# Value products of two successive attention steps issued in the same scheduler step

## The chip, the cores and the metric

The kernel runs on one core of one Trainium2 chip, in one launch. The metric is the device time of a run in microseconds (us); the lower the better. The engines are named as in the profile: PE is TensorE's matmul, PEld its weight load, DVE is VectorE, ACT is ScalarE, POOL is GpSimd, SP is SyncE.

## The reference, cut to what matters

Two encoder layers of width 1024 over 1024 positions. Layer 0 mixes by two groups of 8 heads of 64 value columns, latent attention (MLA) and stick-breaking attention; layer 1 mixes by 16 heads of chunked band attention. A SwiGLU block follows each mixer. Everything is float32. The change touches the three attentions alone:

```python
# MLA: block-causal softmax attention
p_a = softmax(where(chunk_ok, s_a, -inf));  out_a = p_a @ v_a

# stick-breaking: no softmax, a reverse running sum over the keys
log_keep = where(before, log_sigmoid(-z), 0)
log_between = cumsum(log_keep, reverse=True) - log_keep
w_b = where(before, exp(log_sigmoid(z) + log_between), 0);  out_b = w_b @ v_b

# band: own 64-wide chunk and the 8 chunks before it, with a learned bias
p = softmax(where(valid, scores + bias, -inf));  o = p @ v
```

## The kernel before, in words

Each attention handles two heads at once (index `e`) and half the positions at once (`hf`, 512 queries as the columns of a matmul). Along the keys it goes in steps of 128 (`j`): `sb_step`, `mla_attend` and `band_attend` each make one step per block of keys. On or near the diagonal a step covers 384, 256 or 128 of the 512 columns, and stick-breaking goes through the blocks from the last to the first.

A step has stages. Its first stage multiplies keys with queries (scores, in a two-bank PSUM tile `z`) and leaves exponentials in an SBUF tile `a`. Its last stage is the **value product**, `weighted` (L815 to L819): one matmul per head with the tile `a` as the moving operand and 64 value columns as the weights, so that the two heads write the two halves of the 128 partitions of one PSUM bank `o`, which collects all steps of a head pair and half. Stick-breaking has a middle stage, `weights()`: L904, L907 and L909 form the running sum on PE, DVE L915 subtracts it, ACT L916 takes the exponential. The softmax attentions add their exponentials into a tile `b` (L1060: POOL, for the last pairs DVE), and `soft_finish` ends a head pair and half: a matmul with ones for the denominators (L1076), ACT L1078 and L1079, DVE L1080, L1081 and L1082.

`step` holds a list of pending stages. Each call first issues the next stage of every earlier step, oldest first, then the first stage of its own. How many empty stages stand before the last one sets its **lag**: with `LAG` = 2 the weights of a stick-breaking step are issued two calls after its scores and its outputs two calls after that; a band value product is issued two calls after its scores, an MLA one four (`soft_step(2 * LAG, ...)`). Between calls `weave` issues a quota of **fill**: dense three-part matmuls of the next projections or of the output projection (L274, L275, L276), with their weight splits (`rest`, L242). `with_max` puts the row maxima of the next head pair between the steps (MLA: PE L1037, DVE L1039; band: PE L1163, DVE L1166; both end in `neg_max_rows`, L1018 and L1021).

The order in which the calls issue instructions is what the tile scheduler is given; the scheduler then sets the order on each engine, within the dependences and the buffers. Each engine runs its own order strictly from front to back. PSUM has two banks `mm` for fill, two pairs `z`, two banks `o`. The tile `a` has four buffers in layer 0 and three in the band.

In the trace stick-breaking lies between about 86 and 420 us, MLA between 430 and 650, the band between 1422 and 1896. The SwiGLU blocks and the projections around them make up the rest.

Of the kernel before, what the change touches and what calls it, by code (L numbers as in the profile page):

```python
# [30 lines left out]
LAG = 2  # L31
# [119 lines left out]
class Trunk:  # L151
# [711 lines left out]
    def sb_step(self, p, hf, j, proj, vt, st, o_d):  # L863
# [8 lines left out]
        cs = slice(c0, HALF)  # L872
# [55 lines left out]
                nc.sync.dma_start(o_d[hf][4 + p], ot)  # L928

        idle = [lambda: None] * (LAG - 1)  # L930
        self.step(scores, *idle, weights, *idle, outputs)

# [106 lines left out]
        self.neg_max_rows(m2, hf + 1, [qs[e][hf][0][96:100, :] for e in range(2)])  # L1041
        yield

    def soft_step(self, lag, scores, cs, st, vt, j, first, last, dest):
        x = {}

        def front():
            ex = x["ex"] = self.tmp("a")
            scores(ex)
            if first:  # L1050
                st["ex"] = ex
            else:
                old = st["ex"]
                if "esum" not in st:
                    st["esum"] = self.tmp("b")
                    if cs.start:
                        self.nc.scalar.copy(st["esum"][:, :, 0:cs.start], old[:, :, 0:cs.start])
                else:
                    old = st["esum"]
                self.eng("dve" if dest[2] else "pool").tensor_tensor(st["esum"][:, :, cs], old[:, :, cs], ex[:, :, cs],  # L1060
                                                                     ALU.add)

        def back():
            if first:
                st["o"] = self.out_bank()
            self.weighted(st["o"], vt, j, x["ex"], cs, first, last)
            if last:
                self.soft_finish(st["o"], st["esum"], *dest)

        self.step(front, *[lambda: None] * (lag - 1), back)  # L1070

    def soft_finish(self, o, esum, row, k, keep):
        nc = self.nc
# [16 lines left out]
    def mla_attend(self, p, hf, proj, vt, o_d):  # L1090
        nc = self.nc
        mm = nc.tensor.matmul
        qs, ks = proj
        st = {}
        nj = 4 * hf + 4
        for j in range(nj):
            kh, r = divmod(j, 4)
            bs = slice(r * P, (r + 1) * P)
            diag = kh == hf
            cs = slice(r * P if diag else 0, HALF)  # L1100
            kr = 104 if diag else 100

            def scores(ex, kh=kh, bs=bs, cs=cs, kr=kr):
                z = self.banks()
                for e in range(2):
                    qh, ql = qs[e][hf]
                    kth, ktl = ks[e][kh]
                    mm(z[:, e, cs], kth[0:kr, bs], qh[0:kr, cs], start=True, stop=False)  # L1108
                    mm(z[:, e, cs], kth[0:96, bs], ql[0:96, cs], start=False, stop=False)
                    mm(z[:, e, cs], ktl[0:96, bs], qh[0:96, cs], start=False, stop=True)  # L1110
                nc.scalar.activation(ex[:, :, cs], z[:, :, cs], AF.Exp, scale=96 ** -0.5)

            self.soft_step(2 * LAG, scores, cs, st, vt, j, j == 0, j == nj - 1, (o_d[hf], p, p == 3))
            yield 1.0 if not diag else 1.0 - 0.25 * r


# [56 lines left out]
    def band_attend(self, p, hf, proj, tk, vt, o_d):  # L1173
        nc = self.nc
        mm = nc.tensor.matmul
        qs, ks = proj
        st = {}
        order = [0, 1, 2, 3] if hf == 0 else [3, 4, 5, 6, 7, 2, 1, 0]
        for n, j in enumerate(order):
            kh, r = divmod(j, 4)  # L1180
            bs = slice(r * P, (r + 1) * P)
            i0, i1 = max(j, 4 * hf), min(j + 4, 4 * hf + 3)
            cs = slice((i0 - 4 * hf) * P, (i1 - 4 * hf + 1) * P)
            xs = slice((i0 - j) * P, (i1 - j + 1) * P)

            def scores(ex, kh=kh, bs=bs, cs=cs, xs=xs):
                z = self.banks()
                for e in range(2):
                    mm(z[:, e, cs], ks[e][kh][0][:, bs], qs[e][hf][0][:, cs], start=True, stop=False)  # L1189
                    mm(z[:, e, cs], ks[e][kh][1][0:68, bs], qs[e][hf][1][0:68, cs], start=False, stop=True)  # L1190
                nc.vector.tensor_tensor(ex[:, :, cs], z[:, :, cs], tk[:, :, xs], ALU.add)  # L1191
                nc.scalar.activation(ex[:, :, cs], ex[:, :, cs], AF.Exp)  # L1192

            self.soft_step(LAG, scores, cs, st, vt, j, n == 0, n == len(order) - 1, (o_d[hf], p, p == 7))
            yield 1.0 - 0.25 * (3 - i1 + i0)

    def with_max(self, steps, maxes, skip, every=1):
# [279 lines left out]
```

## Time and profile before

| | us |
|---|---|
| time, median of 3 runs | 2613.88 (2611.87 to 2614.07) |
| the profiled execution's own time | 2617.44 |
| its span | 2615.4 |
| outside the span | 2.0 |
| mean granted TensorE clock | 0.988 |

The span goes from the first to the last instruction of the profiled execution. That execution lies 3.6 us above the median of the runs. The rows further down are of two kinds: shares and sums over a stretch, and single instructions in the order of their start. A matmul's duration in a row overlaps with its successor's, so what it costs is the distance from its start to the next start. An instruction's row joins neighbours of the same kind: `x4` on a value product is the two passes of each of two heads, that is one whole step; `x2` is one head, or two matmuls of another kind.

### The profile page before, as it was taken

The page shows a single profiled execution, that of the slowest core. Times are in us where ns is not written, and L with a number is a line of the kernel's source. Part 1 is how long each engine was busy: PE and PEld are TensorE (multiplying, and loading weights), DVE is VectorE, ACT ScalarE, POOL GpSimd, SP SyncE. Part 2 cuts the span into 40 slices and gives each one's busy share as a digit, 9 for nine tenths or more (in the row PEclk, how much of TensorE's full clock was granted, in tenths as well). Part 3 has the DMA queues.
Part 4 walks back from the last instruction along what each step waited for, and adds up shares of the span by engine and source line. Part 5 has one row for each costly group of instructions (what it writes and reads, how often), then busy time and mean ns, then how long its engine had stood idle before and what let it go on. Part 6 is the DMA issues. An engine that isn't in the chain of part 4 may idle for free.

```text
span 2615.4 us, 33607 instructions
## 1 busy us (share of the span) xinstructions
PE 2523.4 (96%) x11758; PEld 1945.9 (74%) x11758; DVE 1911.0 (73%) x3072; ACT 1169.3 (45%) x2028; POOL 520.4 (20%) x489
## 2 busy tenths in 40 slices
PE   7999999999989999999999999999999999999997
PEld 6766765557878888887887766676777888888776
DVE  6888887775886666677666777777688666667775
ACT  4776676454444434433253333334444443443224
POOL 3333324663000000000022333335300000000004
PEclk9999999999999999999999999999999999999999
DMA  4221100125434334476642222222543434447561
GB/s 137 61 63 53 53 17 29 35 69 160 150 121 141 112 134 145 150 261 215 206 152 67 73 82 80 70 69 89 173 161 119 142 109 137 142 151 258 204 213 69
DMA packets 178856, 318.65 MB, mean 122 GB/s; under 512 B 20480, under 2 KB 36736, under 8 KB 178688
## 3 DMA queue, kind: packets, MB, share of 16 engines
q1 hardware_dynamic: 178688, 316.51, 36.7%
q8 instruction: 93, 1.52, 0.2%
q14 instruction: 75, 0.61, 0.1%
HBM read 221.53 MB, written 84.41 MB: 117 GB/s over the span
## 4 chain that ended last, share of the span: by engine, by line
PE 70%; DVE 12%; issue 2%; ACT 1%; DMA 1%; SPq 0%; DVEq 0%; ACTq 0%
PE z L74 24%; PE mm L74 14%; PE o L74 6%; PE mm L274 5%; PE mm L275 5%; PE mm L276 5%; PE o L819 3%; DVE u L74 2%; DVE f L1081 2%; PE z L1189 1%; PE z L1163 1%; PE z L1190 1%; DVE u L297 1%; PE z L1076 1%; PE z L1108 1%
## 5 line engine op out<-in xcount | busy, mean ns | idle before, releaser
L74 PE MATMUL z<-u,wh 128*128 128x512 f32 x992 | 312.6, 396 | 20.9 <-DVE u L74 13.0
L74 PE MATMUL z<-u,vh 128*128 128x512 f32 x992 | 308.0, 392 | 0.0
L274 PE MATMUL mm<-u,wh 128*128 128x512 f32 x720 | 291.6, 405 | 2.5 <-DVE u L699 1.2
L275 PE MATMUL mm<-u,wh 128*128 128x512 f32 x720 | 284.6, 395 | 1.4 <-DVE u L242 1.4
L276 PE MATMUL mm<-u,wl 128*128 128x512 f32 x720 | 283.8, 394 | 0.0
L242 POOL TENSOR_TENSOR wl<-wr,wh 128x512 fp32r<-128x512 f32 (+2 forms) x95 | 122.7, 1298 | 803.9 <-ACT wh L237 735.3
L74 PEld LDWEIGHTS z<-u,wh 128*128 128x128 f32 x992 | 188.4, 191 | 65.2 <-ACT wh L74 18.0
L74 PE MATMUL mm<-u,wh 128*128 128x512 f32 x720 | 222.5, 390 | 0.0
L74 PEld LDWEIGHTS z<-u,vh 128*128 128x128 f32 x992 | 187.6, 189 | 40.3 <-issue 1.0
L74 PE MATMUL z<-u,wl 128*128 128x512 f32 x496 | 195.5, 394 | 0.0
L74 PE MATMUL z<-u,vl 128*128 128x512 f32 x496 | 193.4, 390 | 0.0
L274 PEld LDWEIGHTS mm<-u,wh 128*128 128x128 f32 x720 | 135.6, 188 | 62.5 <-issue 33.3
L819 PE MATMUL o<-a,u 128*64 128x512 f32 (+3 forms) x768 | 172.3, 485 | 0.3 <-ACT a L1192 0.3
L275 PEld LDWEIGHTS mm<-u,wh 128*128 128x128 f32 x720 | 135.8, 189 | 32.6 <-issue 8.3
L276 PEld LDWEIGHTS mm<-u,wl 128*128 128x128 f32 x720 | 135.6, 188 | 32.2 <-issue 3.7
L74 PEld LDWEIGHTS mm<-u,wh 128*128 128x128 f32 x720 | 135.2, 188 | 28.9 <-issue 1.0
L74 PE MATMUL mm<-u,vh 128*128 128x512 f32 x496 | 152.7, 389 | 0.0
L242 POOL TENSOR_TENSOR u<-wr,u 128x512 fp32r<-128x512 f32 x8 | 10.9, 1373 | 673.6 <-ACT u L237 673.6
L74 PE MATMUL mm<-u,wl 128*128 128x512 f32 x360 | 140.1, 389 | 0.0
L1192 ACT ACTIVATE a<-a 128x1024 f32<-128x1024 f32 (+3 forms) x96 | 70.6, 738 | 155.4 <-DVE a L1191 155.1
L1060 POOL TENSOR_TENSOR b<-b,a 128x512 f32<-128x512 f32 (+3 forms) x80 | 110.5, 1381 | 135.9 <-ACT a L1192 120.4
L1191 DVE TENSOR_TENSOR a<-z,bias 128x1024 f32<-128x1024 f32 (+3 forms) x96 | 78.7, 823 | 79.5 <-PE z L1190 65.5
(246 smaller groups left out, 5972.3 us busy)
## 6 DMA issues: line engine op xcount, KB each, us to landing
u<-f_t SPq DMA_DIRECT2D x144, 256.0 KB, 5.2
vr<-in_w_up SPq DMA_DIRECT2D x88, 256.0 KB, 4.0
wr<-in_w_gate SPq DMA_DIRECT2D x88, 256.0 KB, 3.5
f_t<-x SPq DMA_DIRECT2D x72, 256.0 KB, 2.0
wr<-in_w_out SPq DMA_DIRECT2D x64, 256.0 KB, 3.0
f_t<-e SPq DMA_DIRECT2D x54, 256.0 KB, 3.5
ld<-f SPq DMA_DIRECT2D x54, 256.0 KB, 5.2
h<-u SPq DMA_DIRECT2D x48, 256.0 KB, 2.3
```

The source lines that it names most:

```text
L74: return lambda *a, **k: self.tc.keep_in_program_order(f(*a, **k))
L242: self.eng(eng).tensor_tensor(lo, src, hi.bitcast(F32), ALU.subtract)
L274: mm(out, wh, xh, start=first, stop=False, skip_group_check=onto)
L275: mm(out, wh, xl, start=False, stop=False, skip_group_check=onto)
L276: mm(out, wl, xh, start=False, stop=last, skip_group_check=onto)
L297: self.eng(eng).tensor_tensor(acc, acc, sq, ALU.add)
L819: self.nc.tensor.matmul(o[rh, cs], vt[j // 4][:, j % 4, rh], w[:, e, cs], start=first, stop=last)
L1060: self.eng("dve" if dest[2] else "pool").tensor_tensor(st["esum"][:, :, cs], old[:, :, cs], ex[:, :, cs], ALU.add)
L1076: nc.tensor.matmul(den[64 * e:64 * e + 64, :], self.ones[:, 0:64], esum[:, e, :], start=True, stop=True)
L1081: nc.vector.scalar_tensor_tensor(r, t, 2.0, r, ALU.add, ALU.mult)
L1191: nc.vector.tensor_tensor(ex[:, :, cs], z[:, :, cs], tk[:, :, xs], ALU.add)
L1192: nc.scalar.activation(ex[:, :, cs], ex[:, :, cs], AF.Exp)
```

## The change

Three attentions get a lag that depends on the parity of the step, so that the value products of two successive steps are issued in the same call of `step`.

- Stick-breaking: the outputs of an even `j` lose one of their empty stages. As `j` runs downwards, the outputs of an odd `j` and of the even `j` after it fall into one call.
- MLA: `soft_step` gets the step number; an odd step loses one empty stage, an even one stays at lag 4, an odd one goes from 4 to 3.
- Band: the lag given is `LAG + 1`; even steps go from 2 to 3, odd ones stay at 2.

```diff
--- before.py
+++ after.py
@@ -928,7 +928,7 @@
                 nc.sync.dma_start(o_d[hf][4 + p], ot)
 
         idle = [lambda: None] * (LAG - 1)
-        self.step(scores, *idle, weights, *idle, outputs)
+        self.step(scores, *idle, weights, *idle[(j + 1) % 2:], outputs)
 
 
 
@@ -1041,7 +1041,7 @@
         self.neg_max_rows(m2, hf + 1, [qs[e][hf][0][96:100, :] for e in range(2)])
         yield
 
-    def soft_step(self, lag, scores, cs, st, vt, j, first, last, dest):
+    def soft_step(self, n, lag, scores, cs, st, vt, j, first, last, dest):
         x = {}
 
         def front():
@@ -1067,7 +1067,7 @@
             if last:
                 self.soft_finish(st["o"], st["esum"], *dest)
 
-        self.step(front, *[lambda: None] * (lag - 1), back)
+        self.step(front, *[lambda: None] * (lag - 1 - n % 2), back)
 
     def soft_finish(self, o, esum, row, k, keep):
         nc = self.nc
@@ -1110,7 +1110,7 @@
                     mm(z[:, e, cs], ktl[0:96, bs], qh[0:96, cs], start=False, stop=True)
                 nc.scalar.activation(ex[:, :, cs], z[:, :, cs], AF.Exp, scale=96 ** -0.5)
 
-            self.soft_step(2 * LAG, scores, cs, st, vt, j, j == 0, j == nj - 1, (o_d[hf], p, p == 3))
+            self.soft_step(j, 2 * LAG, scores, cs, st, vt, j, j == 0, j == nj - 1, (o_d[hf], p, p == 3))
             yield 1.0 if not diag else 1.0 - 0.25 * r
 
 
@@ -1191,7 +1191,7 @@
                 nc.vector.tensor_tensor(ex[:, :, cs], z[:, :, cs], tk[:, :, xs], ALU.add)
                 nc.scalar.activation(ex[:, :, cs], ex[:, :, cs], AF.Exp)
 
-            self.soft_step(LAG, scores, cs, st, vt, j, n == 0, n == len(order) - 1, (o_d[hf], p, p == 7))
+            self.soft_step(n, LAG + 1, scores, cs, st, vt, j, n == 0, n == len(order) - 1, (o_d[hf], p, p == 7))
             yield 1.0 - 0.25 * (3 - i1 + i0)
 
     def with_max(self, steps, maxes, skip, every=1):
```

No instruction is added or removed. On PE 204 runs of adjacent value products become 150, from stick-breaking to the band; in the SwiGLU blocks nothing moves. Three places show how.

**PE, band, second half of a head pair, two successive steps near its end.** `a_13221` is the tile of a step of 384 columns, `a_13289` that of the next step, of 256. Before, nine dense matmuls and the scores of another step stand between their products:

```order
L819 MATMUL o_13218<-a_13221,u_12118 64x384 x2
L1189 MATMUL z_13322<-u_12564,u_12688 128x128
L1190 MATMUL z_13322<-u_12565,y_12689 128x128
L1189 MATMUL z_13322<-u_12569,u_12694 128x128
L1190 MATMUL z_13322<-u_12570,u_12695 128x128
L1163 MATMUL z_13341<-u_13190,u_13010 128x128
L1163 MATMUL z_13341<-u_13196,u_13015 128x128
...
L819 MATMUL o_13218<-a_13289,u_12118 64x256 x2
L1189 MATMUL z_13358<-u_12564,u_12637 128x384
```

In the change:

```order
L1189 MATMUL z_13320<-u_12562,u_12685 128x128
L1190 MATMUL z_13320<-u_12563,y_12686 128x128
L1189 MATMUL z_13320<-u_12567,u_12691 128x128
L1190 MATMUL z_13320<-u_12568,u_12692 128x128
L1163 MATMUL z_13339<-u_13190,u_13010 128x128
L1163 MATMUL z_13339<-u_13196,u_13015 128x128
...
L276 MATMUL mm_13274<-wh_13264,u_11806 128x256
L819 MATMUL o_13284<-a_13218,u_12118 64x384 x2
L819 MATMUL o_13284<-a_13289,u_12118 64x256 x2
L1189 MATMUL z_13358<-u_12562,u_12637 128x384
```

The product of 384 columns has moved back past the scores and the nine dense matmuls, and stands directly before that of 256.

**PE, band, first half of the next head pair, around a row maximum.** `a_13480` (before) and `a_13478` (change) are the same step, of 512 columns, and `a_13536` is the next, of 384; the L1163 rows are row maxima of the head pair after. Before:

```order
L1163 MATMUL z_13553<-u_13247,u_13122 128x128
...
L276 MATMUL mm_13573<-u_11777,wl_13491 128x512
L819 MATMUL o_13586<-a_13480,u_12827 64x512 x2
L1189 MATMUL z_13590<-u_13010,u_13190 128x256
...
L1163 MATMUL z_13603<-u_13241,u_13117 128x256
L1163 MATMUL z_13603<-u_13247,u_13122 128x256
L275 MATMUL mm_13573<-u_11862,wh_13496 128x512
L276 MATMUL mm_13573<-u_11861,wl_13497 128x512
L819 MATMUL o_13586<-a_13536,u_12827 64x384 x2
```

In the change:

```order
L1163 MATMUL z_13553<-u_13244,u_13120 128x128
...
L274 MATMUL mm_13573<-u_11833,wh_13494 128x512
L1189 MATMUL z_13587<-u_13010,u_13190 128x256
...
L275 MATMUL mm_13573<-u_11862,wh_13494 128x512
L276 MATMUL mm_13573<-u_11861,wl_13495 128x512
L819 MATMUL o_13614<-a_13478,u_12827 64x512
L1163 MATMUL z_13600<-u_13238,u_13115 128x256
L1163 MATMUL z_13600<-u_13244,u_13120 128x256
L819 MATMUL o_13614<-a_13478,u_12827 64x512
L819 MATMUL o_13614<-a_13536,u_12827 64x384 x2
```

The product of 512 columns has moved back behind the dense matmuls; its two heads stand apart, with two row-maximum matmuls between them, and the second head is followed directly by both heads of the 384 step. Ahead of the score L1189 (`z_13590` and `z_13587`), counted from the row maximum `z_13553`, 13 dense matmuls stand now; before, it was 9 and the product.

**PE, stick-breaking, near the end of the second half of the first head pair.** `z_1436` is the running sum of the step whose exponential goes into `a_1334`; `a_1268` (before) and `a_1270` (change) are the step before it. Before:

```order
L909 MATMUL z_1436<-c_1341,masks 128x512 x2
...
L276 MATMUL mm_1427<-u_304,wl_1424 128x512
L819 MATMUL o_1104<-a_1268,u_526 64x512 x2
L274 MATMUL mm_1427<-u_331,wh_1423 128x512
...
L274 MATMUL mm_1427<-u_358,wh_1423 128x512
L904 MATMUL z_1475<-c_1410,masks 128x128 x2
...
L883 MATMUL z_1485<-u_874,u_1085 128x384
L275 MATMUL mm_1427<-u_359,wh_1423 128x512
...
L276 MATMUL mm_1427<-u_385,wl_1424 128x512
L819 MATMUL o_1104<-a_1334,u_526 64x512 x2
```

In the change:

```order
L909 MATMUL z_1436<-c_1341,masks 128x512 x2
L275 MATMUL mm_1429<-u_305,wh_1425 128x512
...
L883 MATMUL z_1445<-u_874,u_1085 128x256
L276 MATMUL mm_1429<-u_304,wl_1426 128x512
L274 MATMUL mm_1429<-u_331,wh_1425 128x512
L819 MATMUL o_1104<-a_1270,u_526 64x512 x2
L904 MATMUL z_1480<-c_1412,masks 128x128 x2
L909 MATMUL z_1480<-c_1413,masks 128x128
L819 MATMUL o_1104<-a_1334,u_526 64x512 x2
L909 MATMUL z_1480<-c_1413,masks 128x128
```

Only two rows stand between the product of `a_1334` and that of the step before, and between it and the L909 on which its exponential depends there are nine dense matmuls, four score matmuls and one L909 less.

## Rows read from the trace of the kernel before

**Rows 1.** The head of the page: the span, then busy time, share of the span and instructions of each engine.

```profile
span 2615.4 us, 33607 instructions
PE 2523.4 (96%) x11758; PEld 1945.9 (74%) x11758; DVE 1911.0 (73%) x3072; ACT 1169.3 (45%) x2028; POOL 520.4 (20%) x489
```

**Rows 2.** Windows of stick-breaking, MLA and the band: from:to in us, length, then busy time (and instructions) of PE, PEld, DVE, ACT and POOL, the granted TensorE clock as a share of full speed, the DMA share and GB/s.

```profile
86.00:346.00 260.00, 253.19 (x1225) 181.29 (x1221) 224.39 (x281) 180.87 (x258) 93.89 (x121) 1.00 0.20 56
440.00:650.00 210.00, 203.63 (x896) 127.58 (x896) 143.12 (x171) 95.62 (x149) 114.32 (x79) 0.99 0.25 79
1422.00:1796.00 374.00, 363.91 (x1972) 259.27 (x1970) 274.45 (x563) 137.21 (x244) 138.07 (x136) 1.00 0.25 76
```

**Rows 3.** The timeline of PE in stick-breaking: start, duration, engine, line, operation, tiles, shape and count. A whole step of 512 columns between dense matmuls.

```profile
303.03 0.39 PE L275 MATMUL mm<-u,wh 128*128 128x512 f32 x1
303.26 0.39 PE L276 MATMUL mm<-u,wl 128*128 128x512 f32 x1
303.57 1.08 PE L819 MATMUL o<-a,u 128*64 128x512 f32 x4
304.58 0.50 PE L904 MATMUL z<-c,masks 128*128 128x256 f32 x2
```

**Rows 4.** The same view in the band: a whole step of 128 columns and the matmul after it.

```profile
1517.25 0.44 PE L819 MATMUL o<-a,u 128*64 128x128 f32 x4
1517.62 0.39 PE L1189 MATMUL z<-u,u 128*128 128x256 f32 x1
```

**Rows 5.** The same view at the end of the band: a step of 256 and one of 128 columns side by side (`x8`), between dense matmuls.

```profile
1830.55 0.39 PE L274 MATMUL mm<-u,wh 128*128 128x512 f32 x1
1830.77 0.39 PE L275 MATMUL mm<-u,wh 128*128 128x512 f32 x1
1831.09 0.87 PE L819 MATMUL o<-a,u 128*64 128x256 f32 x8
1831.89 0.50 PE L276 MATMUL mm<-u,wl 128*128 128x512 f32 x1
1832.23 0.40 PE L274 MATMUL mm<-u,wh 128*128 128x512 f32 x1
```

**Rows 6.** The same view in stick-breaking: one head of a step of 512 columns (`x2`) that stands alone.

```profile
139.57 1.07 PE L819 MATMUL o<-a,u 128*64 128x512 f32 x2
140.57 0.50 PE L276 MATMUL mm<-u,wl 128*128 128x512 f32 x1
```

**Rows 7.** The timeline of POOL, DVE and PE in the first half of a band head pair, up to a stall of PE. In brackets the engine's idle time before the instruction and what ended it.

```profile
1535.71 1.84 POOL L1060 TENSOR_TENSOR b<-a,a 128x768 f32<-128x768 f32 x1 [5.93 <-ACT a L1192]
1535.80 2.30 DVE L1081 SCALAR_TENSOR_TENSOR f<-f,f 128x512 f32<-128x512 f32 x1
...
1537.81 1.08 PE L819 MATMUL o<-a,u 128*64 128x512 f32 x4
...
1539.23 0.68 DVE L1166 CUSTOM_DVE_ANT_0 z<-z,bias 128x512 f32<-128x512 f32 x1
...
1540.03 0.39 PE L1189 MATMUL z<-u,u 128*128 128x256 f32 x1 [1.14 <-DVE m L1166]
```

**Rows 8.** The same view in the second half of the same head pair.

```profile
1565.34 0.68 DVE L242 TENSOR_TENSOR wl<-wr,wh 128x512 fp32r<-128x512 f32 x1
...
1567.91 1.85 POOL L1060 TENSOR_TENSOR b<-b,a 128x768 f32<-128x768 f32 x1 [4.48 <-ACT a L1192]
...
1568.31 2.00 DVE L242 TENSOR_TENSOR wl<-wr,wh 128x512 fp32r<-128x512 f32 x1 [0.82 <-ACT wh L237]
...
1570.36 0.39 PE L275 MATMUL mm<-wl,u 128*128 128x256 f32 x1 [0.76 <-DVE wl L242]
```

**Rows 9.** The waits of PE between 1422 and 1896 us, over the whole band: us in total, times, longest us.

```profile
PE z L1189 <- DVE m L1166: 5.7, 5, 1.2
PE mm L275 <- DVE wl L242: 4.3, 6, 0.8
```

**Rows 10.** The timeline of PE, DVE and POOL in MLA, at the end of a head pair and half.

```profile
511.27 4.12 DVE L1081 SCALAR_TENSOR_TENSOR f<-f,f 128x512 f32<-128x512 f32 x1
...
512.50 5.12 POOL L1060 TENSOR_TENSOR b<-b,a 128x1024 f32<-128x1024 f32 x2
...
516.51 0.44 PE L1108 MATMUL z<-u,u 104*128 104x384 f32 x1 [2.37 <-DVE m L1039]
```

**Rows 11.** The window that begins with the last of these rows; columns as in rows 2.

```profile
516.50:518.90 2.40, 2.39 (x10) 2.17 (x12) 0.00 (x0) 0.40 (x1) 1.11 (x1) 0.59 0.29 109
```

**Rows 12.** The waits of PE between 86 and 650 us; columns as in rows 9.

```profile
PE z L1108 <- DVE m L1039: 3.6, 4, 2.4
PE z L1037 <- DVE m L1039: 1.5, 2, 0.9
```

**Rows 13.** The timeline of PE and ACT in stick-breaking: twice the last matmul of the running sum of a step, and the exponential of the same step, which follows from it through DVE L915.

```profile
145.15 0.62 PE L909 MATMUL z<-c,masks 128*128 128x512 f32 x2
...
147.06 1.06 ACT L916 ACTIVATE a<-a 128x1024 f32<-128x1024 f32 x1 [2.21 <-DVE a L915]
...
187.08 0.62 PE L909 MATMUL z<-c,masks 128*128 128x512 f32 x2
...
194.45 1.06 ACT L916 ACTIVATE a<-a 128x1024 f32<-128x1024 f32 x1 [0.42 <-DVE a L915]
```

**Rows 14.** All waits of PE directly ahead of a value product that an exponential of stick-breaking ended, over the whole span: us in total, times.

```profile
  ACT a L916: 0.4, 1
```

## The prediction

> **What bounds the kernel now.** I read the head of the page first: PE is busy for 2523.4 of 2615.4 us, DVE for 73%, ACT for 45% [rows 1]. Then the windows of the three attentions, since nothing moves elsewhere. PE is busy for 97% in each of them, at a granted clock of 0.99 to 1.00, that is at its 2.4 GHz level [rows 2]. DVE is close behind in stick-breaking, 224.4 of 260 us. What PE leaves idle there is little: 6.8, 6.4 and 10.1 us in the three windows. So the change can gain in two ways, by a cheaper order of the same matmuls on PE, or by shorter waits, and it can lose by both. Last I read the timeline around value products for what one costs, and the waits of PE for what could go.
>
> **What a value product costs on PE.** A whole step of 512 columns takes 304.58 - 303.57 = 1.01 us from start to start [rows 3], one of 128 columns 1517.62 - 1517.25 = 0.37 [rows 4]. That is 0.64 us for 384 columns, 1.67 ns a column, and 0.157 us that do not depend on the columns. A step of 256 and one of 128 side by side take 1831.89 - 1831.09 = 0.80 [rows 5]; 0.157 and 384 columns make just that, while apart they would take 0.58 + 0.37. So the 0.157 is paid once for a group of adjacent products. The way in and out costs too. A dense matmul takes 0.22 to 0.23 to the next start, but 0.31 to 0.32 when a value product follows [rows 3, 5], 0.09 more; the first matmul behind a group takes 0.34 [rows 5], 0.11 more. **A group costs 0.157 + 0.09 + 0.11, about 0.35 us, beside its columns.**
>
> One head alone costs as much as both: 140.57 - 139.57 = 1.00 us for one head of 512 columns [rows 6]. The two heads write different halves of the partitions and run beside each other when they are adjacent. **A step whose heads are torn apart pays its columns twice, 1.67 ns for each.**
>
> **The change, part by part.** No instruction is added or removed, so the PE term is a count over the whole order of both programs.
>
> Groups: 204 become 150 (as listed with the change). 54 x 0.35 = **-18.9 us**. The first place of order is the clean case: the product of 384 columns joins that of 256. I take the bounds from the same rows: 0.157 a group, if the way in and out were not saved, gives -8.5; 0.37 gives -20.
>
> A rule of the Trainium skill bears on this term, in TensorEngine Tiling (Array Packing), section Tiling Modes: changing the tiling mode drains the TensorE. The 128*64 tiles of the value products against 128*128 around them [rows 3] would be such a change. The page has no price; TensorE: Matmul & The Clock Gate, section Single matmul latency, gives (398 + N)/2.4 ns for a lone matmul at the fast clock, of which 166 ns do not depend on N. Two such drains a group, an estimate from that page, would be 0.33 us and 54 of them -17.9, so 2605.3 where the rows give 2604.3. The rows decide, and the sum goes by them.
>
> Torn heads: of the 96 pairs of steps that the change means to join, 7 stood whole in one group before and 48 do in the change; 26 share a group but leave one head ahead of it, as in the second place of order, where row maxima stand between the heads of the 512 step; 22 stay apart. Adding up the columns that run with one head alone gives 7,936 columns paid twice before and 12,928 in the change. 4,992 x 1.67 ns = **+8.3 us**. Both counts together give -10.6: stick-breaking -6.2, MLA -0.5, band -3.9.
>
> Waits in the band: **+1 us**. In the first half of a head pair PE stalls before L1189 for 1.14 us, until the row maximum L1166 frees its bank. L1166 is late because DVE's L1081 took 2.30 us where POOL's L1060 ran beside it [rows 7]. In the change 13 dense matmuls cover this instead of 9 and a product: 13 x 0.23 = 2.99 against 9 x 0.23 + 1.01 + 0.20 = 3.28, so the stall grows by 0.3, in seven head pairs +2.0. In the second half PE waits 0.76 for a weight split L242, which took 2.00 instead of 0.68 behind the same kind of POOL add [rows 8]. In the change's order on DVE the score addition L1191 stands before the first of these splits; POOL's add can begin up to one split, 0.68, sooner. The split still waits 0.82 for ACT [rows 8], so I take a third, 0.22, and with six such waits [rows 9] -1.3. Bounds: the second gain at its full 6 x 0.68 = -4 without the first loss, and the first loss twice over, +4.
>
> Waits in stick-breaking: **+3 us**. The product of an even step comes one call sooner, and its exponential may not be there. From the start of the last L909 to the end of L916 it takes 147.06 + 1.06 - 145.15 = 2.97 us in a quick case and 8.43 in a slow one [rows 13]. By the order, with the prices above, PE has between 2.6 and some 10 us of other work in between. The third place of order is near the least: three dense, four scores, a product. 13 steps fall short of the quick case, by 4.7 us in sum. Before, PE waited for L916 directly ahead of a value product only once, 0.4 us [rows 14]. I take +3, since a product that waits also gives the next exponential time; bounds 0 and +7, if some of the short ones are slow cases. Behind a waiting product stand all of PE's later matmuls, the next L904 among them, and through it DVE's L915.
>
> Waits in MLA: **-3 us**. PE waits 3.6 and 1.5 us behind the maxima L1039 [rows 12]. The longest, 2.37 us, came when DVE sat in L1081 for 4.12 us beside POOL's adds of 5.12 [rows 10], and the clock was then 0.59 over 2.4 us [rows 11], 1.0 us more lost: 1.2 GHz for most of it. In the change the closing product and the denominators L1076 come one call sooner than the maxima, and by the order PE has 8.6 instead of 5.0 us of work between them. Bounds: -6 (both waits and the clock) and +2 (L1076 now waits for POOL's last add).
>
> The copy L927 with its transfer L928, and in MLA `soft_finish` with its own, start one call sooner. I cost that at nothing: the output projection reads them long after, and if that cover were gone, it would be a transfer once at the end of the stage. The scratch tile `a` is freed no later than the scores that reuse it.
>
> **Sum:** -18.9 + 8.3 + 1 + 3 - 3 = -9.6 us on 2617.44, the profiled execution's own time: 2607.8. The median of the runs lies 3.6 below it, so I predict 2613.88 - 9.6 = **2604.3 us**.
>
> **The rivals.**
> *The locked engines take it back.* POOL's adds stretch DVE instructions, 0.68 to 2.00 [rows 8], and PE waits for DVE in the band already. A new order need only put one more such instruction behind an add in each of six or seven head pairs: 1.3 x 6.5 = 8.5 us, so 2612.8, no change. For it: every band stall is of this kind [rows 9]. Against it: DVE has 26% of its time free there [rows 2]. The Trainium skill has the rule in SBUF — State Buffer, section Who interferes with whom: a DVE instruction with two SBUF inputs contends with a GpSimd instruction that reads SBUF, and the order of issue decides who blocks. Rows 8 agree with it.
>
> *The sooner products wait (the other sign).* 24 steps of stick-breaking and 24 of MLA have products one call sooner, at the head of PE's queue. At 0.4 us each it is 19 us instead of the 3 taken: +6.4, 2620.3. It decides from (9.6 + 5.2) / 48 = 0.31 us a product above what I take. For it: DVE at 86% in stick-breaking, and the slow chain of 8.43 us. Against it: MLA keeps a lag of 3 calls, and [rows 14].
>
> *All waits shrink too.* At 0.37 a group the PE term is -20 + 8.3 = -11.7; half of the lower bounds of the waits in the band and in MLA, -2 and -3, and none in stick-breaking make it -16.7, so 2597.2. For it: each of these stalls is 1 to 2 us late only [rows 7, 8, 10], and PE gets other work in front of them. Against it: the same DVE and POOL instructions stay.
>
> **How the numbers follow.** About 0.2%, 5.2 us, is what a measurement of this kernel can tell from no change. My forecast has 0.52, of which 0.05 falls short of 0.2%; the locked engines 0.23 (same); the sooner products 0.15 (slower); all waits shrink 0.10. Faster 0.47 + 0.10 = 0.57, same 0.28, slower 0.15. The range goes from 2594 (-20, all of those bounds but 1.7 us) to 2617 (the PE term at its low bound, -0.2, with waits of +3); it leaves out most of the slower case and a little at either end. My forecast's own range is 2599 to 2609.
>
> **What would show it.** The value products in fewer groups with busy time up, not down; around a group 0.31 and 0.34 as before; PE's idle time in the band within 1 or 2 us of before; no 2.4 us stall with a fallen clock in MLA. In stick-breaking waits ahead of value products ended by L916, 3 us in sum. It is wrong if those reach 10 us, if PE's waits for L242 or L1166 grow by more than 5 us, or if a group saves only the 0.157.

## The result, and the profile after

The change made the kernel slower: 2625.55 us median (2622.59 to 2628.41, 5 runs) against 2614.07 (2611.87 to 2615.86, 5 runs), ratio 1.0042, 95% interval 1.003 to 1.0053. That is +11.5 us where -9.6 was forecast; the time lies outside the range. From here on each kernel is compared with the kernel before as it was measured beside it, since that moved between 2613.1 and 2615.2 us from one set of runs to the next.

The profiled execution of the change took 2628.41 us, 11.0 more than that of before. The head of its page and its windows, which answer to [rows 1, 2] (the first window is stick-breaking from the first zero product L923 to the last L909, the same stretch as the one below it of before; the second is MLA):

```profile
span 2626.6 us, 33609 instructions
PE 2521.7 (96%) x11758; PEld 1956.1 (74%) x11758; DVE 1924.2 (73%) x3072; ACT 1170.2 (45%) x2028; POOL 519.0 (20%) x489
```

```profile
85.40:419.70 334.30, 312.90 (x1474) 225.67 (x1472) 288.96 (x353) 233.72 (x352) 115.03 (x137) 0.98 0.16 47
...
440.00:666.00 226.00, 212.72 (x913) 134.31 (x914) 155.12 (x176) 97.70 (x154) 116.06 (x80) 0.97 0.23 74
```

Of before, the same stretch of stick-breaking:

```profile
85.40:415.60 330.20, 316.50 (x1473) 224.09 (x1472) 283.57 (x353) 232.45 (x351) 114.20 (x137) 0.98 0.17 48
```

PE works less, as its busy time says, and yet the end comes later. To see where, I cut every trace at the same instructions: the first L923, the last L909 (the end of stick-breaking), the first SwiGLU matmul L74, the first row maximum L1163 of the second layer, the first L74 after the band, and PE's last matmul. The lengths in us:

| | stick-breaking | MLA | SwiGLU 0 and band projections | band | SwiGLU 1 |
|---|---|---|---|---|---|
| before | 330.2 | 242.5 | 742.4 | 501.9 | 703.1 |
| change | 334.3 | 254.2 | 743.8 | 497.8 | 701.0 |
| difference | +4.1 | +11.7 | +1.4 | -4.1 | -2.1 |

The stretches with SwiGLU hold the same code in all kernels here and came out between 742 and 746 and between 699 and 704 us, so their differences say nothing. The forecast was about -3 in stick-breaking, -3.5 in MLA, -3 in the band. The band did what was forecast; the other two went the other way.

### The profile page after: what moved, and what is told of

It reads as the page before. It is cut to its first block, busy times and chain, and to the rows that moved or that the text cites. A ratio compares the mean times of both kernels' runs of the same rounds, so it can differ in the third digit from the quotient of the medians.

```text
span 2626.6 us, 33609 instructions
## 1 busy us (share of the span) xinstructions
PE 2521.7 (96%) x11758; PEld 1956.1 (74%) x11758; DVE 1924.2 (73%) x3072; ACT 1170.2 (45%) x2028; POOL 519.0 (20%) x489
## 4 chain that ended last, share of the span: by engine, by line
PE 68%; DVE 12%; ACT 2%; issue 2%; DMA 1%; SPq 0%; POOL 0%; DVEq 0%; ACTq 0%; POOLq 0%
PE z L74 24%; PE mm L74 14%; PE o L74 6%; PE mm L274 5%; PE mm L275 5%; PE mm L276 5%; PE o L819 4%; DVE u L74 2%; DVE f L1081 2%; PE z L1189 1%; PE z L1163 1%; PE z L1190 1%; DMA ld<-f 1%; PE z L1076 1%; DVE u L297 1%
## 5 line engine op out<-in xcount | busy, mean ns | idle before, releaser
L74 PE MATMUL z<-u,wh 128*128 128x512 f32 x992 | 312.8, 396 | 20.1 <-DVE u L74 12.1
L74 PE MATMUL z<-u,vh 128*128 128x512 f32 x992 | 309.3, 393 | 0.0
L274 PE MATMUL mm<-u,wh 128*128 128x512 f32 x720 | 288.5, 401 | 2.9 <-DVE f L977 0.8
L242 POOL TENSOR_TENSOR wl<-wr,wh 128x512 fp32r<-128x512 f32 (+2 forms) x95 | 122.3, 1294 | 810.3 <-ACT wh L237 743.4
L74 PEld LDWEIGHTS z<-u,wh 128*128 128x128 f32 x992 | 188.4, 190 | 64.6 <-ACT wh L74 18.3
L74 PE MATMUL mm<-u,wh 128*128 128x512 f32 x720 | 222.5, 390 | 0.0
L74 PEld LDWEIGHTS z<-u,vh 128*128 128x128 f32 x992 | 188.5, 190 | 40.7 <-issue 1.0
L74 PE MATMUL z<-u,wl 128*128 128x512 f32 x496 | 196.1, 395 | 0.0
L74 PE MATMUL z<-u,vl 128*128 128x512 f32 x496 | 193.7, 391 | 0.0
L274 PEld LDWEIGHTS mm<-u,wh 128*128 128x128 f32 x720 | 135.6, 188 | 47.6 <-issue 18.4
L74 PEld LDWEIGHTS mm<-u,wh 128*128 128x128 f32 x720 | 135.2, 188 | 29.0 <-issue 1.0
L74 PE MATMUL mm<-u,vh 128*128 128x512 f32 x496 | 152.7, 389 | 0.0
L242 POOL TENSOR_TENSOR u<-wr,u 128x512 fp32r<-128x512 f32 x8 | 10.9, 1373 | 671.9 <-ACT u L237 671.9
L74 PE MATMUL mm<-u,wl 128*128 128x512 f32 x360 | 140.1, 389 | 0.0
```

The costliest lines, as they stand in the source:

```text
L74: return lambda *a, **k: self.tc.keep_in_program_order(f(*a, **k))
L242: self.eng(eng).tensor_tensor(lo, src, hi.bitcast(F32), ALU.subtract)
L274: mm(out, wh, xh, start=first, stop=False, skip_group_check=onto)
```

## The price of a value product held

The timeline of PE in the band of the change: two whole steps of 512 columns in one group, then the first place of order (384 and 256 columns), then the second place, with the torn heads.

```profile
1519.03 1.94 PE L819 MATMUL o<-a,u 128*64 128x512 f32 x8
1520.89 0.39 PE L1189 MATMUL z<-u,u 128*128 128x256 f32 x1
...
1526.87 1.30 PE L819 MATMUL o<-a,u 128*64 128x384 f32 x8
1528.16 0.44 PE L1189 MATMUL z<-u,u 128*128 128x384 f32 x1
...
1556.81 1.07 PE L819 MATMUL o<-a,u 128*64 128x512 f32 x2
1557.81 0.51 PE L1163 MATMUL z<-u,u 128*128 128x256 f32 x2
1558.25 1.72 PE L819 MATMUL o<-a,u 128*64 128x512 f32 x6
1559.89 0.50 PE L274 MATMUL mm<-u,wh 128*128 128x512 f32 x1
```

From start to start the groups take 1.86, 1.29, 1.00 and 1.64 us; 0.157 plus 1.67 ns a column, with torn heads counted twice, gives 1.86, 1.22, 1.01 and 1.65. The waits of PE in the band, which answer to [rows 9], grew little, and its idle time there went from 12.7 to 12.5 us:

```profile
PE z L1189 <- DVE m L1166: 6.2, 5, 1.2
PE mm L275 <- DVE wl L242: 4.3, 6, 0.8
```

The band's PE term was 33 groups less (-11.5) and 4,608 columns more paid twice (+7.7), -3.9 in all, and the stretch is 4.1 us shorter.

## One part of the change at a time

Three kernels undo two of the three parts each. Against the change, these are the edits: sb_only has the second and the third, mla_only the first and the third, band_only the first and the second.

```diff
-        self.step(scores, *idle, weights, *idle[(j + 1) % 2:], outputs)
+        self.step(scores, *idle, weights, *idle, outputs)
...
-            self.soft_step(j, 2 * LAG, scores, cs, st, vt, j, j == 0, j == nj - 1, (o_d[hf], p, p == 3))
+            self.soft_step(0, 2 * LAG, scores, cs, st, vt, j, j == 0, j == nj - 1, (o_d[hf], p, p == 3))
...
-            self.soft_step(n, LAG + 1, scores, cs, st, vt, j, n == 0, n == len(order) - 1, (o_d[hf], p, p == 7))
+            self.soft_step(0, LAG, scores, cs, st, vt, j, n == 0, n == len(order) - 1, (o_d[hf], p, p == 7))
```

> Only the stick-breaking line of the change; MLA and band keep their old lags. Theory A (each attention carries its own part): the stick-breaking stretch grows by the 3.7 us that the trace of the change shows there (its value products now wait for the causal mask on POOL), MLA and band as before: +3 to +4, about 2618. Theory B (the loss in MLA comes from the shifted end of stick-breaking, through the fill and the weight splits that MLA inherits): +12 to +16, about 2628. Theory of the prediction: -3, about 2611.

> Only the MLA part. Theory A: the MLA stretch grows by 12 us by itself (four stalls of 2.5 to 3 us behind the row maxima and the slower clock after them): about 2626. Theory B: MLA alone is within 3 us of before. Theory of the prediction: -3.5, about 2610.5.

> Only the band part. Theory A and the prediction agree: -3 to -4 us, about 2610. If the band's gain of 4.1 us in the trace of the change rests on the earlier stages' different timing (Theory B), it would be 0 here, about 2614.

Measured, against 2615.22 of before: sb_only 2617.94 (ratio 1.0016, 1.0007 to 1.0025), mla_only 2628.23 (1.0052, 1.0039 to 1.0065), band_only 2610.74 (0.9985, 0.9976 to 0.9994). So +2.7, +13.0 and -4.5 us, +11.2 in sum against +11.5 for the whole change. Each of the three intervals is 2.4 to 3.4 us to either side. Each attention carries its own part (Theory A), and the loss in MLA is not inherited from the stage ahead (Theory B falls).

## MLA: the closing, one call sooner

The waits of PE in the change that answer to [rows 12], from 86 to 660 us:

```profile
PE z L1108 <- DVE m L1039: 7.3, 4, 3.0
PE z L1037 <- DVE m L1039: 4.9, 6, 2.7
```

5.1 us have become 12.2. One of these stalls, by the timeline of DVE, POOL and PE; it answers to [rows 10]:

```profile
513.76 1.27 POOL L242 TENSOR_TENSOR u<-c,u 96x512 fp32r<-96x512 f32 x1
...
514.56 6.38 DVE L1081 SCALAR_TENSOR_TENSOR f<-f,f 128x512 f32<-128x512 f32 x1
514.99 2.39 POOL L1060 TENSOR_TENSOR b<-b,a 128x1024 f32<-128x1024 f32 x1
...
517.33 0.73 POOL L242 TENSOR_TENSOR wl<-wr,wh 128x256 fp32r<-128x256 f32 x1
518.01 2.38 POOL L1060 TENSOR_TENSOR b<-b,a 128x1024 f32<-128x1024 f32 x1
...
520.97 0.69 DVE L977 TENSOR_TENSOR c<-mm,u 32x512 f32<-32x512 f32 x1
521.70 0.69 DVE L1082 TENSOR_TENSOR f<-o,f 128x512 f32<-128x512 f32 x1
522.42 0.68 DVE L978 TENSOR_TENSOR c<-c,c 32x512 f32<-32x512 f32 x1
523.14 0.43 DVE L1039 TENSOR_REDUCE m<-z 128x2 f32<-128x256 f32 x1
...
523.62 0.69 PE L1108 MATMUL z<-u,u 104*128 104x384 f32 x1 [2.47 <-DVE m L1039]
```

L1081 comes while POOL is in a split L242, and POOL then goes through two sums and another split with no gap until 518.01 + 2.38 = 520.39. L1081 ends at 514.56 + 6.38 = 520.94, 0.55 us after that. Behind it on DVE stand L977, L1082, L978 and only then the row maximum L1039, for which PE stands still. Before, at the place of [rows 10], L1082 alone stood between the two:

```profile
515.43 0.69 DVE L1082 TENSOR_TENSOR f<-o,f 128x512 f32<-128x512 f32 x1
516.04 0.42 DVE L1039 TENSOR_REDUCE m<-z 128x2 f32<-128x256 f32 x1
```

So the row maximum is later by 2.3 us of L1081 and by two rotary instructions of 0.7 each. The window from the end of this stall in the change, which answers to [rows 11]:

```profile
523.60:530.40 6.80, 6.78 (x16) 3.61 (x17) 0.69 (x1) 2.61 (x4) 5.44 (x3) 0.50 0.17 57
```

The granted clock is 0.50, the 1.2 GHz level, for 6.8 us, which costs 3.4 us more, so the stall of 2.47 costs 5.9. Two further stalls behind L1039 are of the same kind: 2.98 us at 470.80, behind an L1081 of 6.84, and 2.66 at 577.36, behind a cast L993 of 8.52. Behind each of these two the clock fell for half as long, at a cost of 1.7 us. Over the whole MLA stretch PE is idle for 17.3 instead of 10.5 us, and the three falls cost 6.8 us where the one of before, behind its stall of 2.37, cost 1.7 (516.50 to 520.40 us at 0.56): 6.8 and 5.1 more, which is the 11.7 within 0.2.

In mla_end_late the last MLA step of a head pair and half keeps its lag of 4, against the change:

```diff
-        self.step(front, *[lambda: None] * (lag - 1 - n % 2), back)
+        self.step(front, *[lambda: None] * (lag - 1 - (n % 2 if lag < 4 or not last else 0)), back)
```

> The whole change, but the last step of each MLA head pair and half keeps its lag of 4 calls, so that its closing (denominators L1076, DVE L1080 to L1082) comes as late as before; the other odd steps of MLA stay sooner. Theory A1 (the closing, one call sooner, puts DVE L1081 beside POOL's run of rotary splits and sums, and the row maximum behind it): L1081 back to 1 to 4 us, the stalls behind L1039 back to about 5 us in sum, 9 to 12 us less than the change, about 2615. Theory A2 (the loss in MLA comes from the products of the other odd steps, torn heads and waits for exponentials): at most 3 us less than the change, about 2623 to 2625.

Measured: 2619.02 against 2615.22 of before (1.0016, 1.0008 to 1.0025), +3.8 where the change has +11.5, so 7.7 less where 9 to 12 were expected. The MLA stretch is back at 242.8 us (before 242.5), and the durations of L1081 (min/median/max) are those of before, 678/2300/4122, where the change has 687/2302/6836:

```profile
L1081 DVE SCALAR_TENSOR_TENSOR f<-f,f x24: 676/2300/4126, 465.7 to 1903.6; 128x512 f32<-128x512 f32 x24
```

So the larger part of the loss in MLA is the closing (Theory A1; A2 had at most 3 us less). Three of four odd steps of MLA stay sooner in this kernel, or one of two, and that they cost nothing is not shown by it. PE is idle for 13.1 us in its MLA stretch, against 10.5 before; the stretch is no longer because the granted clock over it is 0.99 instead of 0.98; behind its stall of 2.32 us it stayed at 1.00 (520.70 to 526.00 us). And by the medians 5.6 us of the 13.0 of mla_only remain (+3.8, less the +2.7 and -4.5 of the other two parts), each median with an interval of 2.2 to 3.4 us to either side. bpm_keep, below, finds no such cost.

Whether POOL holds L1081 for its two SBUF operands was tested by giving it one of them from PSUM, in the change and in the kernel before:

```diff
-        den = self.banks()[:, 0, :]
+        zz = self.banks()
+        den, t = zz[:, 0, :], zz[:, 1, :]
...
-        r, t, ot = self.tmp("f"), self.tmp("f"), self.tmp("f")
+        r, ot = self.tmp("f"), self.tmp("f")
```

> The whole change, with one edit in soft_finish: the intermediate t of L1080 goes to the unused second bank of the pair that holds the denominators, so that L1081 reads one operand from PSUM and one from SBUF instead of two from SBUF. Theory A1 (L1081 is held by POOL's run because it reads two SBUF operands): every L1081 takes 0.7 to 0.8 us, also beside POOL; of the MLA stalls behind L1039 those that follow L1081 shrink from about 3 us each to below 1, with the slow clock behind them; 6 to 10 us less than the change, about 2616 to 2620. Rival (POOL's run holds whatever DVE instruction stands there; the next one with two SBUF operands, L978, takes the place): L1081 is quick, L978 takes 4 to 6 us, and the time is within 3 us of the change, about 2623 to 2626.

> The kernel before with the same edit in soft_finish alone (t of L1080 in PSUM). Theory A1: L1081 at 0.7 to 0.8 us instead of up to 4.12; the MLA stall of 2.37 us and its slow clock go (-3), and so do most of the band's stalls before L1189 of 1.14 us behind L1081 and L1166 (-4 to -5): about 2606 to 2609. Rival (something else holds the row maxima): within 2 us of before.

Measured, against 2613.09 of before: after_psum 2606.55 (0.9976, 0.9967 to 0.9985), before_psum 2603.78 (0.9967, 0.9955 to 0.9979). The held instruction (line 1082 in this kernel) takes 0.69 us each of the 24 times in after_psum, and 17 of these begin while POOL is at work:

```profile
L1082 DVE SCALAR_TENSOR_TENSOR f<-z,f x24: 676/691/693, 462.6 to 1892.5; 128x512 f32<-128x512 f32 x24
```

So the hold is shown, and for L1081 it goes by operands. The Trainium skill has this in SBUF — State Buffer, section Who interferes with whom: a DVE instruction with two SBUF inputs contends with a GpSimd instruction that reads SBUF. 0.69 against up to 6.84 us agree. Two SBUF operands are not the only case: L993, held for 8.52 us in the change, is a cast that reads one. The sizes were not as expected. Each against its own before, after_psum is 18.0 us below the change. By the traces, which are 20.7 us apart, 6.4 lie in MLA (254.2 to 247.8) and 15 in the band (497.8 to 482.9), where L1081 of 2.30 us had been ahead of L1166, and stick-breaking is 2.2 longer. In before_psum all the gain is in the band, 501.9 to 490.5; MLA is 1.3 us longer, since its stall of 2.37 us is gone but others have come, the longest of 1.80 before L274, with a fall of the clock behind it. And in MLA the rival holds in part. In after_psum one stall of 3 us is left, behind the next DVE instruction with two SBUF operands, L978:

```profile
558.98 6.82 DVE L978 TENSOR_TENSOR c<-c,c 32x512 f32<-32x512 f32 x1
...
562.88 2.36 POOL L1060 TENSOR_TENSOR b<-b,a 128x1024 f32<-128x1024 f32 x1
...
565.53 2.48 POOL L1060 TENSOR_TENSOR b<-b,a 128x1024 f32<-128x1024 f32 x1 [0.28 <-ACT a L1112]
565.83 0.70 DVE L1081 SCALAR_TENSOR_TENSOR z<-z,f 128x512 f32<-128x512 f32 x1
566.56 0.69 DVE L1082 SCALAR_TENSOR_TENSOR f<-z,f 128x512 f32<-128x512 f32 x1
567.31 0.51 PE L1109 MATMUL z<-u,u 104*128 104x512 f32 x1 [3.04 <-DVE f L1082]
```

L978 came free 0.56 us after the end of POOL's sum at 565.24; L1082 ran beside the next sum, of 2.48 us, and kept its 0.69. PE waits here for L1082 itself: with t in the second bank, the pair of banks is occupied until L1082 has read it, which is the price of the edit. In these kernels the scheduler also orders other instructions anew, so the differences of the whole time hold more than the one instruction.

## Stick-breaking: waits for what PE saves

PE's busy time in the stretch fell by 3.6 us and its idle time rose from 13.7 to 21.4. The waits of PE in sb_only, over stick-breaking, that before did not have or had shorter (before: none for L876, 0.2 for L904 behind L915, none for L904 behind L885):

```profile
PE o L819 <- POOL a L876: 3.4, 4, 1.7
...
PE z L904 <- DVE a L915: 2.2, 3, 1.2
...
PE z L904 <- DVE a L885: 1.1, 1, 1.1
```

The waits of L909 for its splits L242 do not belong here: on DVE and POOL together they went from 3.9 to 3.2 us. The first of the three is the rival of the prediction, at a place that I had not priced: on the diagonal the product waits for the exponential and, behind it, for POOL's causal mask. In the change:

```profile
252.93 0.69 DVE L915 TENSOR_TENSOR a<-a,z 128x512 f32<-128x512 f32 x1
...
254.19 0.63 ACT L916 ACTIVATE a<-a 128x512 f32<-128x512 f32 x1
254.37 1.85 POOL L242 TENSOR_TENSOR c<-b,c 128x384 fp32r<-128x384 f32 x1 [1.71 <-ACT c L892]
...
256.87 0.63 POOL L876 TENSOR_SCALAR_AFFINE_SELECT a<-a 128x256 f32<-128x256 f32 x1
...
257.55 0.65 PE L819 MATMUL o<-a,u 128*64 128x256 f32 x4 [1.63 <-POOL a L876]
```

L916 was done at 254.82, but the mask stood behind a split L242 and a fill L845 on POOL until 256.87.

In sb_offdiag, against before, only the even steps off the diagonal come sooner:

```diff
-        self.step(scores, *idle, weights, *idle, outputs)
+        self.step(scores, *idle, weights, *idle[0 if diag else (j + 1) % 2:], outputs)
```

> Only the stick-breaking part, and only for even steps off the diagonal (two of the four in the second half of each head pair), where no causal mask on POOL stands between the exponential and the value product. Theory S1 (the part loses because products on the diagonal wait for POOL's mask L876): no waits for L876 ahead of products beyond before's, and a gain of 1 to 3 us against before, about 2612 to 2614. Theory S2 (the loss comes from DVE, which now has L915 in front of other work): as sb_only, +2 to +3, about 2617.

Measured: 2615.91 against 2613.09 of before (1.0011, 1.0002 to 1.002), +2.8. The waits for L876 ahead of products are gone from the list, as S1 had it, but no gain came, as S2 had it: L904 now waits for L915 for 5.7 us in 7 times, against 0.2 once, and the stretch is 332.1 us, 1.9 above before. The mask is one way in which the saved time is lost, not the only one. The next pair relieved DVE of L888; before_no888 is before with this edit, sb_no888 is sb_only with it:

```diff
-            nc.vector.tensor_tensor(t[:, :, cs], t[:, :, cs], zc[:, :, cs], ALU.max)
```

> The kernel before without DVE L888, the maximum of the softplus with its argument in stick-breaking (this leaves a part of the computation out): 48 DVE instructions of up to 1.3 us less. It is the partner of sb_no888; by itself stick-breaking is expected shorter by 5 to 20 us if DVE limits it, and by 0 to 3 us if PE does.

> The stick-breaking part of the change alone, also without L888. Against before_no888: theory D (the part loses because DVE, 86% busy, sets the pace, so that what PE saves turns into waits for it): with DVE relieved the PE term of -6 shows, -3 to -6 us. Theory C (the products one call sooner wait for the chain of exponential and mask itself, whatever DVE's load): as sb_only, +1 to +4 us.

Measured: before_no888 2611.8 and sb_no888 2610.32, against 2614.75 of before (0.9986, 0.9977 to 0.9996, and 0.9979, 0.9968 to 0.9989): the part costs -1.5 us where sb_only had +2.7, between the two expectations, and the intervals overlap. The stretch itself speaks more clearly, though from one execution each. It is 329.9 and 322.8 us, 7.1 less with the part, against 330.2 and 334.6, 4.4 more, at full load; 1.7 of the 7.1 are the clock, which stood at 0.50 for 13.7 us in the first and 10.2 in the second. The same stretch came out between 330.0 and 330.7 us in the five kernels that share the old code, and between 334.3 and 336.5 in the four with the new one. PE's idle time in it is 15.7 and 15.8 us, where at full load the part raised it from 13.7 to 20.9. So in these traces what PE saves is kept once DVE has less to do, for theory D. Yet the stretch of before_no888 is no shorter than that of before, so DVE does not limit the old order, and sb_no888 still has 5.9 us of waits for L876. What share each of the two has stays open.

## Heads kept together, and a better kernel

By the order the change pays 12,928 columns twice, before 7,936. High priority for the second head's matmul puts it directly behind the first:

```diff
         for e in range(2):
...
-            self.nc.tensor.matmul(o[rh, cs], vt[j // 4][:, j % 4, rh], w[:, e, cs], start=first, stop=last)
+            if e:
+                with self.tc.high_priority():
+                    self.nc.tensor.matmul(o[rh, cs], vt[j // 4][:, j % 4, rh], w[:, e, cs], start=first, stop=last)
+            else:
+                self.nc.tensor.matmul(o[rh, cs], vt[j // 4][:, j % 4, rh], w[:, e, cs], start=first, stop=last)
```

> The whole change, and the matmul of the second head of each value product is given to the scheduler with high priority, so that it stands directly behind the first: by the order no step has its heads torn apart (12,928 columns paid twice become none) and 150 groups become 141. Theory T1 (torn heads cost 1.67 ns a column and a group 0.35 us, as the prediction took them): -21.5 and -3.2 us against the change, about 2601. Theory T2 (PE waits for DVE and POOL anyway, and what the products save turns into waits): less than half of it, -5 to -10 us, about 2616 to 2620.

> The kernel before with the same high priority for the second head: 7,936 columns paid twice become none, 204 groups become 182. Theory T1: -13.2 and -7.7, about 2593. Theory T2: -4 to -9, about 2606 to 2610. The distance between this run and after_keep is what the change does where heads aren't torn: by T1 41 groups less, -14.4, against its added waits of about +22 us, so +6 to +9.

Measured, against 2613.42 of before: after_keep 2606.82 (0.9978, 0.9962 to 0.9994), -6.6 where the change has +11.5, so 18.1 less; before_keep 2598.67 (0.9944, 0.993 to 0.9958), -14.8. T1 had -24.7 and -20.9, T2 at most half. Seven tenths of what PE saves arrive. The distance between the two is +8.2, in the +6 to +9 expected; the intervals are 4 us to either side.

The parts that gained were then put together:

> Only the band part of the change, with the PSUM edit of soft_finish. If the gains add (band part -4.5 by its own run, PSUM edit -5 to -8 by theory A1): -9 to -12, about 2602 to 2606. If the band part's gain and the edit's are the same stalls: no better than the better of the two alone, about 2609.

> The band part of the change, the PSUM edit of soft_finish, and the high priority for the second head: 12,800 columns paid twice become none, 169 groups become 153, against band_psum. Theory T1: -21.3 and -5.6, about 2573. Theory T2: half or less, 2586 or more.

> The kernel before with the PSUM edit and the high priority for the second head, without any part of the change; the partner of band_psum_keep. If the joining of two steps still pays where heads stay together, this is slower than band_psum_keep by the 29 groups between them (182 against 153) at 0.35 us, 10 us, about 2583; if the joining pays nothing, it is the same, about 2573.

> The whole change with the PSUM edit and the high priority for the second head. If the stick-breaking part and the early closing of MLA keep their price there (+3 and +6, as sb_only and after_psum showed against before and band_psum): 8 to 10 us more than band_psum_keep, about 2582. If both prices came from torn heads: within 2 us of it, about 2573.

> As band_psum_keep, with the MLA part of the change added but for the last step of each head pair and half, which keeps its old lag. If the MLA part loses only by its early closing and by L1081: 0 to -3 us against band_psum_keep (3 groups less, 1 us, and fewer waits). If the odd products one call sooner cost waits of their own: +3 us or more.

| | median us | before, measured beside it | ratio, 95% interval | band stretch | MLA stretch |
|---|---|---|---|---|---|
| band_psum | 2599.68 | 2613.09 | 0.9945, 0.9933 to 0.9958 | 483.3 | 243.8 |
| before_psum_keep | 2585.55 | 2614.75 | 0.9881, 0.9868 to 0.9895 | 485.1 | 232.3 |
| band_psum_keep | 2572.83 | 2613.42 | 0.9846, 0.983 to 0.9862 | 475.1 | 231.3 |
| bpm_keep | 2573.29 | 2613.42 | 0.9847, 0.9831 to 0.9863 | 475.3 | 229.9 |
| after_psum_keep | 2586.42 | 2614.75 | 0.9885, 0.9872 to 0.9899 | 475.1 | 236.1 |

The gains of the band part and of the PSUM edit add: -4.5 and -9.3 alone, -13.4 together in band_psum. Joining pays by itself: with heads whole, the band part of the change makes the band 10.0 us shorter (485.1 to 475.1) for 29 groups, 0.35 us each. The second place of order, a step of 512 columns with row maxima and a step of 384 behind it, looks like this in band_psum_keep (the lines of `weighted` are 823 for the first head and 821 for the second here; one row each, two passes):

```profile
1517.71 0.64 PE L823 MATMUL o<-a,u 128*64 128x512 f32 x1
1517.72 0.64 PE L821 MATMUL o<-a,u 128*64 128x512 f32 x1
1518.19 0.59 PE L823 MATMUL o<-a,u 128*64 128x512 f32 x1
1518.20 0.59 PE L821 MATMUL o<-a,u 128*64 128x512 f32 x1
1518.72 0.50 PE L1168 MATMUL z<-u,u 128*128 128x256 f32 x2
1519.15 0.54 PE L823 MATMUL o<-a,u 128*64 128x384 f32 x1
```

The second head starts 0.01 us after the first and costs nothing: 1.01 us for the step that took 1.00 + 0.85 in the change. From band_psum to band_psum_keep the time fell by 27.2 us, each against its own before, where T1 had 26.9; by the traces 23.9 of it lie in the three attentions. The MLA part without its early closing adds nothing (2573.29 against 2572.83), and stick-breaking and the early closing together keep a price: each against its own before, after_psum_keep is 12.3 us above band_psum_keep (8 to 10 were expected), by the traces 6.1 in stick-breaking (332.9 against 326.8) and 4.9 in MLA. band_psum_keep is 41 us below the kernel before.

## Why the prediction was wrong, point by point

Of the error of 21 us, 15 lie in MLA (-3.5 forecast, +11.7 measured) and 7 in stick-breaking (-3.2 and +4.1).

- *Price of a group and of a torn head:* right. Rows of the change agree to 0.1 us, the band, where both terms weigh most, came out at -4.1 to -4.5 against -2.9, and 29 groups less made the band 10.0 us shorter where heads are whole.
- *Waits in the band, +1:* right in size by luck. The two waits grew by 0.5 us in sum and another of 1.3 went. Neither of the two opposed terms of 2.0 and 1.3 appeared as worked out.
- *Waits in MLA, -3:* the step that failed, wrong in sign, and the largest error. I gave PE more work between the closing and the row maximum, which came as counted, and put the earlier `soft_finish` at nothing. That kept DVE's L1081 at the length that it had in the row. But L1081 moved in time too, into a run of POOL, and grew from 2.73 and 4.12 us to 6.84 and 6.38; three and two rotary instructions of 0.7 us (of L976 to L978) came between it and the row maximum, and a cast L993 was held for 8.52. Together this was more than the 3.6 us of cover that PE gained. With the closing put back (mla_end_late) 7.7 us of the loss go. The 1.0 us for the clock was priced as a thing that goes; it was 1.7, since the fall went on beyond the window of [rows 11], and became 6.8.
- *Waits in stick-breaking, +3:* too small. Idle time grew by 7.7 us, just above the upper bound of 7. I compared the product's cover with the quick chain L909 to L916, but waits for L916 ahead of a value product are 0.7 us in 2 times in the change, against 0.4 in [rows 14]. I left out the mask L876 that follows on the diagonal (2.8 us), and that earlier products leave L904 with less cover of its own (behind L915 and L885 3.1 us, before 0.2).
- *PE term in stick-breaking, -6.2:* 3.6 of it show as less busy time.
- *The rivals:* the locked engines had the mechanism, but I placed it in the band, at 1.3 us a time, where it hardly came; it came in MLA with 3 us and a slow clock behind each. The sooner products had the right sign by luck: they were priced as waits of products for exponentials. In stick-breaking products did wait, for the mask, for a third to a half of the added idle time, in MLA hardly at all.

## What to carry to other kernels

Matmuls of 64 output columns that fill different halves of the partitions should be given to the scheduler so that they stay adjacent: a torn pair paid its columns twice here, and a group cost 0.35 us however many products it held. When a step is moved in time, look up for each of its instructions which other engine can hold it and what that engine does at the new time; a duration read in a row holds for its neighbours in that row only. An instruction with two SBUF operands, ahead of one for which PE waits, is better given one from PSUM while POOL is busy, if the bank that it occupies meanwhile can be spared.

## What the runs showed of the hardware

POOL's hold does not have to end with one of its instructions. Where POOL went from one to the next without a gap, a DVE instruction could stand through several of them: L1081 for 6.38 and 6.84 us and, in the change, a cast for 8.52, at 0.4 to 0.7 us of their own work:

```profile
567.73 8.52 DVE L993 CAST u<-u 32x512 fp32r<-32x512 f32 x1
```

It does not always happen. In the kernel before, POOL also passed from a sum to a split without a gap, and there L1081 came free after 2.73 us, with 1.71 us for the split:

```profile
461.35 2.38 POOL L1060 TENSOR_TENSOR b<-b,a 128x1024 f32<-128x1024 f32 x1
461.55 2.73 DVE L1081 SCALAR_TENSOR_TENSOR f<-f,f 128x512 f32<-128x512 f32 x1
463.69 1.71 POOL L242 TENSOR_TENSOR u<-c,u 96x512 fp32r<-96x512 f32 x1
```

What decides between the two stays open. One operand in PSUM lifted the hold on L1081 fully, 0.69 us in all 24 cases.

Behind the change's PE stalls of 2.98, 2.47 and 2.66 us the granted clock fell to 0.50, the 1.2 GHz level, and each fall cost 1.7 or 3.4 us more. The length of the stall alone does not tell whether it falls: behind 2.37 us it fell in the kernel before, while behind the same 2.37 us in sb_offdiag it stayed at 1.00 (516.20 to 522.00 us).
